# A fused hybrid block on one core: a bias added by VectorE, and sums of the expert units moved

## The chip, the core and the metric

The kernel runs on one core of a Trainium2 chip, as one program. The metric is the device time of one execution in microseconds; the kernel before takes 536.47 us, the median of 3 runs (535.53 to 536.54).

## The reference

One layer on 512 tokens of width 1024, all in float32:

```
mod = silu(c) @ w_ada + b_ada                  # 6 vectors of 1024: sh_a, sc_a, g_a, sh_f, sc_f, g_f
h   = rms_norm(x) * (1 + sc_a) + sh_a
proj = h @ w_in                                # -> conv value, conv gate, c_q, c_kv, k_rope
y_conv = silu(layer_norm(depthwise_conv31(val * sigmoid(gate))))
y_attn = attention(q, k, v from c_q, c_kv; 8 heads, chunk-causal)
x   = x + g_a * (concat(y_conv, y_attn) @ w_out)
h2  = rms_norm(x) * (1 + sc_f) + sh_f
y   = sum over the 2 chosen of 32 experts: gate_e * (silu(h2 @ Wg_e) * (h2 @ Wu_e)) @ Wd_e
out = x + g_f * y
```

`mod` is the conditioning; its last 4096 values (g_a, sh_f, sc_f, g_f) are what the first part of the change touches. The experts' weights are 3 MB each, 32 experts.

## The kernel before

Order. From the end of the first stage on, TensorE, VectorE, ScalarE and (until the experts) GpSimd run in the order in which the program text issues their instructions, and so does SyncE's queue of DMA triggers. A DMA that ScalarE triggers stands in ScalarE's order with its computations.

Stages. First the input projection of all tokens (`sweep1`). Then, while the convolution is prepared, the rest of the conditioning is computed in steps between other work: `ada_rest` (L569) makes two groups of 2048 values. A group is 8 products of the replicated silu(c) with a 128x2048 slice of `w_ada`, each as four products of 512 columns at four row positions of one PSUM bank (L574), then the bias as four more products of an identity column with the row tile `brow` (L581; a float32 product shows as two instructions, so 8 per group), then ScalarE copies the bank to a tile (L586). SyncE stores the four rows (L602) and reads them back in other shapes. `load_brow` (L565) is a DMA that ScalarE triggers; the first stands in the program after GpSimd's splittings of w_q_b and w_kv_b (L549, L552) and before the convolution's pairs, the second right after the first group's bias products. The `w_ada` slices come through a ring of 4 buffers.

The bank comes from the tag `f`, which has 2 buffers. Just before the first group, `conv_pair(1)` holds both: value and gate of a convolution tile. `conv_in` (L308) reads the gate with ScalarE's tanh (L312) and then the value with VectorE (L315). VectorE meanwhile works through the convolution's taps (L346).

`ada_rest`'s steps are called by `fill`: the first group's first step follows the first quarter of `conv_pair(2)`, its last step stands ahead of the last quarter's rest of `conv_pair(3)`; the second group runs between the q, k, v products and transpositions.

Then attention, the output projection with routing, and the experts. The experts' tokens are worked in 12 units of up to 128 rows (`Unit`, L1412), 2 or 4 experts each. A unit: transposition of the gathered rows (L1425), gate and up products (`gate_up`, L1451), silu and multiplication (L1454, L1456), transposition of the result (`turn`, L1463, copied by ScalarE at L1465), down products (`down`, L1477), scaling by gate and g_f with a split in a high part (ScalarE, L1481) and a low part (L1482), for two halves of 512 columns. `combine` (L1485) adds finished units to the residual: 8 steps, each a few products with a one-hot matrix into a bank (L1495) and a VectorE sum (L1498); with `store`, the result goes out by DMA (L1500), by SyncE and ScalarE in turn. From unit 5 on (`SOON`), four steps of the unit before stand in the middle of `gate_up`, four after `turn`. Before `turn` stands the next unit's transposition with its VectorE work (L1439, L1440). SyncE streams all weights (L1008) through 4 and 15 buffers and waits where a buffer is still read.

Of the kernel before, what the change touches and what calls it, by code (L numbers as in the profile page):

```python
# [12 lines left out]
F32 = mybir.dt.float32  # L13
# [4 lines left out]
OP = mybir.AluOpType  # L18
# [23 lines left out]
def hybrid_block(ctx: ExitStack, tc: tile.TileContext, A, out, dbg=None, stop=None):  # L42
    nc = tc.nc
    pe, act, dve, pool, sp = nc.tensor, nc.scalar, nc.vector, nc.gpsimd, nc.sync
# [42 lines left out]
    def nm(s):  # L87
        uid[0] += 1
        return f"{s}_{uid[0]}"
# [4 lines left out]
    def S(shape, dt=F32):  # L94
        return slots.tile(shape, dt, tag="s", name=nm("s"))

    def T(shape=(128, 512), dt=F32):
        return tmp.tile(list(shape), dt, tag="t", name=nm("t"))
# [4 lines left out]
    def acc(shape=(128, 512), dt=F32):  # L103
        return psum.tile(list(shape), dt, tag="acc", name=nm("acc"), bufs=4)

    def fb(shape=(128, 512), dt=F32):
        return psum.tile(list(shape), dt, tag="f", name=nm("f"), bufs=2)
# [4 lines left out]
    def C(shape, dt=F32, name=None, uname=None):  # L112
        return const.tile(list(shape), dt, tag=name, name=uname or name)
# [31 lines left out]
    def xrow(tt):  # L145
        return X[tt // 2][:, tt % 2, :]
# [23 lines left out]
    ident = C([128, 128], name="ident")  # L170
# [30 lines left out]
    def crep(j):  # L201
        return cs[:, j:j + 1].to_broadcast([128, 32])
# [62 lines left out]
    def sweep1(j):  # L265
        q, jj = j // 2, j % 2
        wh, wl = whl[q]
        hh, hl = hTh[j // 4][:, j % 4, :], hTl[j // 4][:, j % 4, :]
        for a in range(2):
            cc = slice(a * 128, (a + 1) * 128)  # L270
            mm3(pcv[a], wh[:, jj, cc], wl[:, jj, cc], hh, hl, j == 0, j == 7)
            yield
        for tt in range(4):
            cc = slice(tt * 128, (tt + 1) * 128)
            mm3(pcc[tt][:, :416], hh[:, cc], hl[:, cc], wh[:, jj, 256:], wl[:, jj, 256:], j == 0, j == 7)
            yield

    def run(g, n=100):
        for _ in range(n):
            if next(g, 0) == 0:  # L280
                break
# [5 lines left out]
    rp = S([128, 2048])  # L287
# [162 lines left out]
    for j in range(8):  # L450
        g = sweep1(j)
# [42 lines left out]
    def load_next():  # L494

        n = stream[0]
        stream[0] += 1
        if n < 16:
            t = ada_f[n // 8, n % 8] = W([128, 2048])
            sp.dma_start(t, w_ada[:, n % 8, 2048 + 2048 * (n // 8):4096 + 2048 * (n // 8)])  # L500
        elif n < 20:
            part, hf = (n - 15) % 2, (n - 16) // 2
            t = wout[part, hf] = W([128, 4, 512])
            sp.dma_start(t, wov[:, 4 * part:4 * part + 4, 512 * hf:512 * hf + 512])
# [11 lines left out]
    for tt in range(4):  # L516
        p = pcc[tt]
# [5 lines left out]
    for tt in range(4):  # L523
        p = pcc[tt]
# [34 lines left out]
    H2n = C([128, 8], name="H2n")  # L559
    rows = [dram.tile([4, 512], F32, tag=f"row{i}", name=f"row{i}") for i in range(2)]  # L560

    brow = rp[:4, 1536:2048]

    def load_brow(i):
        act.dma_start(brow, A["b_ada"][0, 2048 + 2048 * i:4096 + 2048 * i].rearrange("(a b) -> a b", b=512))  # L565

    load_brow(0)

    def ada_rest():  # L569
        for grp in range(2):  # L570
            p = fb()
            for j in range(8):
                for g in range(4):
                    pe.matmul(p[32 * g:32 * g + 32, :], crep(j), ada_f[grp, j][:, 512 * g:512 * g + 512],  # L574
                              start=(j == 0), stop=False, tile_position=(0, 32 * g), skip_group_check=True)
                if j < 7:
                    load_next()
                    store_rows(stream[0])
                    yield
            for g in range(4):  # L580
                pe.matmul(p[32 * g:32 * g + 32, :], ident[:4, g:g + 1].to_broadcast([4, 32]), brow,  # L581
                          start=False, stop=True, tile_position=(0, 32 * g), skip_group_check=True)
            if grp == 0:
                load_brow(1)
            s = T()
            act.copy(s, p)  # L586
            load_next()
            rows_due.append((stream[0] + RD[grp], grp, s))
            yield
        store_rows(100)  # L590
        yield
        store_rows(200)
# [27 lines left out]
    def conv_pair(t):  # L620
        wh, wl = pair_w[t]
        pv = [acc(), acc()] if t > 1 else [fb(), fb()]
        for a in range(2):
            for j in range(8):
                yield
                mm3(pv[a], wh[:, a, j, :], wl[:, a, j, :], hTh[j // 4][:, j % 4, :], hTl[j // 4][:, j % 4, :], j == 0, j == 7)
        conv_in(t, pv[0], pv[1])
# [12 lines left out]
    g = conv_pair(1)  # L640
# [4 lines left out]
    g = conv_pair(2)  # L645
# [9 lines left out]
    g = conv_pair(3)  # L655
# [80 lines left out]
    def qkv_fill():  # L736
        for i in range(24):
            fill(FQ[i % len(FQ)])
            yield
# [64 lines left out]
    g = qkv_fill()  # L804
# [186 lines left out]
    for kind in ORDER:  # L991
        n_ = sum(k[0] == kind for k in units)
# [41 lines left out]
    ga, gf = gw[:, 0], gw[:, 1]  # L1034
# [283 lines left out]
    for tt in range(4):  # L1318
        step = lambda k=1, tt=tt: run(rs_[tt], k)
        places = lambda tt=tt: (place(tt, 0, routed[tt][5]), tt < 3 and by_expert(tt, 0, routed[tt][5]))  # L1320
        n = 5 * tt + (5 if tt < 3 else 8)
        for d, f in ((0, lambda tt=tt: x2_part(tt, 0)), (D0, step), (D1, step)):
            at(n + d, f)
        if tt < 3:
            n = 31 + 8 * tt
# [86 lines left out]
    class Unit:  # L1412
# [53 lines left out]

        def down(self, eng=pool):

            n = self.n
            self.yhl = S([128, 2, 1024], F32R)  # L1470
            for hf in range(2):
                hs = slice(512 * hf, 512 * hf + 512)
                o = acc()
                for c in range(2):
                    for o_, w_, i in self.pieces:
                        w = self.weights(i, "d")
                        pe.matmul(o[o_:o_ + w_, :], self.aT[:, n * c + o_:n * c + o_ + w_], w.t[:, c, hs],  # L1477
                                  start=(c == 0), stop=(c == 1), tile_position=(0, o_), skip_group_check=True)
                yf = T()
                dve.scalar_tensor_tensor(yf[:n], o[:n], self.gate, gf[:n, hs], op0=OP.mult, op1=OP.mult)  # L1480
                act.copy(self.yhl[:n, 0, hs], yf[:n])  # L1481
                eng.tensor_tensor(self.yhl[:n, 1, hs], yf[:n], self.yhl[:n, 0, hs].bitcast(F32), op=OP.subtract)  # L1482
                yield

    def combine(us, banks=(fb,) * 4, store=False):  # L1485

        for u_ in us:
            if not u_.ot:
                u_.one_hot()
        for hf in range(2):  # L1490
            for tt in range(4):
                o = banks[tt]()
                for m, u_ in enumerate(us):
                    for k in range(2):
                        pe.matmul(o, u_.ot[:u_.n, tt * 128:(tt + 1) * 128], u_.yhl[:u_.n, k, 512 * hf:512 * hf + 512],  # L1495
                                  start=(m == 0 and k == 0), stop=(m == len(us) - 1 and k == 1))
                xr = xrow(tt)[:, 512 * hf:512 * hf + 512]
                dve.tensor_tensor(xr, xr, o, op=OP.add)  # L1498
                if store:
                    (act if tt % 2 else sp).dma_start(out[0, tt * 128:(tt + 1) * 128, 512 * hf:512 * hf + 512], xr)  # L1500
                yield
# [34 lines left out]
    cur = start(0)  # L1536
# [5 lines left out]
    SOON = 5  # L1542
    comb, done, side, prev = iter(()), [], over_table(), None
    for n_ in range(len(units)):
        last = n_ == len(units) - 1
        cur.gate_up(lambda: n_ >= SOON and run(comb, 4))
        if n_ == 1:
            run(gate)
        nxt_u = start(n_ + 1)
        if nxt_u:  # L1550
            nxt_u.complete()
        if prev:
            run(prev.down())
            done.append(prev)
        cur.turn()
        if n_ < SOON:
            if len(done) == 2:
                comb, done = combine(done), []
            run(comb, 4)
        else:  # L1560
            run(comb)
            if done:
                run(combine(done))
            if last:
                comb = combine([cur], (fb, fb, tr, tr), True)
                cur.one_hot()
                run(cur.down(dve))
                run(comb)
                break
            run(cur.down())  # L1570
            comb, done = combine([cur]), []
        if n_ > 1:
            run(side, 1)
        r_ = [Wt[e, part].room for part in (0, 1) for e in units[n_][2]]
        if n_ < 3:
            r_.remove("s")
        if prev:
            r_ += [Wt[e, "d"].room for e in units[n_ - 1][2]]
        if n_ >= SOON:
            r_ += [Wt[e, "d"].room for e in units[n_][2]]  # L1580
        room += r_
        loads_upto(len(keys))
        prev, cur = cur if n_ < SOON else None, nxt_u
# [124 lines left out]
```

## Time and profile before

| | |
|---|---|
| median of 3 runs | 536.47 us |
| the profiled execution's own time | 534.46 us |
| its span, first to last instruction | 532.9 us |
| TensorE busy | 486.2 us (91%) |
| VectorE, ScalarE, GpSimd busy | 289.0, 178.3, 124.4 us |
| granted TensorE clock, mean | 0.984 of full speed |
| moved by DMA | 154.42 MB, 290 GB/s |

The profile names PE (TensorE), PEld (its weight loads), DVE (VectorE), ACT (ScalarE), POOL (GpSimd) and SP (SyncE); a q behind the name is the engine's queue. "tile<-tiles" names what is written and read; `f`, `acc` and `tr` are PSUM banks. A bracket at the end of a timeline row is idle time of that engine before the row, and what ended it.

### The profile page before, as it was taken

The page shows a single profiled execution, that of the slowest core. Times are in us where ns is not written, and L with a number is a line of the kernel's source. Part 1 is how long each engine was busy: PE and PEld are TensorE (multiplying, and loading weights), DVE is VectorE, ACT ScalarE, POOL GpSimd, SP SyncE. Part 2 cuts the span into 40 slices and gives each one's busy share as a digit, 9 for nine tenths or more (in the row PEclk, how much of TensorE's full clock was granted, in tenths as well). Part 3 has the DMA queues.
Part 4 walks back from the last instruction along what each step waited for, and adds up shares of the span by engine and source line. Part 5 has one row for each costly group of instructions (what it writes and reads, how often), then busy time and mean ns, then how long its engine had stood idle before and what let it go on. Part 6 is the DMA issues. An engine that isn't in the chain of part 4 may idle for free.

```text
span 532.9 us, 8170 instructions
## 1 busy us (share of the span) xinstructions
PE 486.2 (91%) x2891; PEld 272.9 (51%) x2891; DVE 289.0 (54%) x655; ACT 178.3 (33%) x389; POOL 124.4 (23%) x118
## 2 busy tenths in 40 slices
PE   4899999999999898999998999999998999999982
PEld 4768975535644365788874343444433333223331
DVE  2447779957948675551556233436455454133544
ACT  4232744016575556821534422111201212021110
POOL 2311580007654543200000113012120212001100
PEclk9989999999999989999999999999999999999997
DMA  8999539985960262276968999999999999999934
GB/s 270 302 320 310 156 122 325 368 330 174 247 228 9 73 237 92 75 271 220 361 197 321 292 355 371 317 405 413 398 415 408 411 413 411 410 417 409 414 162 164
DMA packets 57859, 154.42 MB, mean 290 GB/s; under 512 B 7337, under 2 KB 26937, under 8 KB 51664
## 3 DMA queue, kind: packets, MB, share of 16 engines
q1 hardware_dynamic: 53232, 143.89, 75.6%
q10 hardware_dynamic: 2688, 5.92, 3.0%
q0 software_dynamic: 1888, 4.00, 2.3%
q8 instruction: 25, 0.41, 0.3%
q14 instruction: 26, 0.21, 0.1%
HBM read 150.97 MB, written 4.77 MB: 292 GB/s over the span
## 4 chain that ended last, share of the span: by engine, by line
PE 69%; DVE 13%; DMA 6%; ACT 4%; SPq 3%; issue 2%; POOL 1%; DVEq 0%; ACTq 0%; POOLq 0%
PE acc L1451 18%; PE acc L1477 9%; PE f L1495 8%; PE acc L116 5%; PE acc L118 4%; PE acc L117 4%; DVE s L1498 3%; DVE dw L346 2%; PE f L334 2%; DMA s<-in_w_ada_dram 2%; PE tr L1425 2%; DMA w<-in_w_ada_dram 2%; PE f L574 2%; PE acc L899 2%; DMA xg<-t 2%
## 5 line engine op out<-in xcount | busy, mean ns | idle before, releaser
L1451 PE MATMUL acc<-s,gw 128*32 128x512 f32 (+1 forms) x408 | 92.5, 597 | 0.0
L1498 DVE TENSOR_TENSOR s<-s,f 128x512 f32<-128x512 f32 x76 | 49.6, 685 | 35.9 <-PE f L1495 35.9
L116 PE MATMUL acc<-s,s 128*128 128x512 f32 (+3 forms) x160 | 63.2, 395 | 1.0 <-DVE s L774 1.0
L1495 PE MATMUL f<-s,t 128*128 128x512 f32 x184 | 54.4, 425 | 8.8 <-DVE s L1498 5.4
L118 PE MATMUL acc<-s,s 128*128 128x512 f32 (+3 forms) x160 | 58.8, 368 | 0.0
L117 PE MATMUL acc<-s,s 128*128 128x512 f32 (+3 forms) x160 | 58.8, 367 | 0.0
L346 DVE SCALAR_TENSOR_TENSOR dw<-s,cwh,dw 128x512 f32<-128x512 f32 x60 | 49.8, 844 | 1.2
L1451 PEld LDWEIGHTS acc<-s,gw 128*32 128x32 f32 (+1 forms) x408 | 24.6, 122 | 46.7 <-issue 44.8
L1451 PE MATMUL acc<-w,gw 128*32 128x512 f32 (+1 forms) x120 | 48.2, 622 | 0.0
L1482 POOL TENSOR_TENSOR s<-t,s 128x512 fp32r<-128x512 f32 x22 | 28.2, 1281 | 85.1 <-ACT s L1481 79.1
L1495 PEld LDWEIGHTS f<-s,t 128*128 128x128 f32 x184 | 30.0, 188 | 33.0 <-DVE s L1498 16.9
L1477 PE MATMUL acc<-s,t 128*64 128x512 f32 (+1 forms) x184 | 44.5, 598 | 0.0
L1454 ACT ACTIVATE t<-acc 128x256 f32<-128x256 f32 x12 | 4.6, 384 | 111.5 <-PE acc L1451 111.5
L116 PEld LDWEIGHTS acc<-s,s 128*128 128x128 f32 x160 | 30.2, 189 | 14.8 <-issue 7.9
L1456 DVE TENSOR_TENSOR t<-t,acc 128x256 f32<-128x256 f32 x12 | 5.1, 421 | 58.4 <-ACT t L1454 58.4
L1481 ACT CAST s<-t 128x512 fp32r<-128x512 f32 x24 | 14.8, 618 | 63.7 <-DVE t L1480 56.7
L1409 POOL DMA_INDIRECT s<-xg,sidx x11 | 11.7, 1060 | 98.1 <-PE tr L1425 61.7
L118 PEld LDWEIGHTS acc<-s,s 128*128 128x128 f32 x160 | 30.1, 188 | 4.1
L117 PEld LDWEIGHTS acc<-s,s 128*128 128x128 f32 x160 | 30.2, 189 | 3.3 <-issue 0.2
L1480 DVE SCALAR_TENSOR_TENSOR t<-acc,rt,gw 128x512 f32<-128x512 f32 x24 | 18.0, 750 | 25.0 <-PE acc L1477 25.0
L871 ACT ACTIVATE t<-acc,sm,qs 128x128 f32<-128x128 f32 (+3 forms) x32 | 19.7, 616 | 21.6 <-DVE sm L869 18.4
L868 DVE TENSOR_REDUCE sm<-acc 128x1 f32<-128x128 f32 (+3 forms) x32 | 15.5, 486 | 19.8 <-PE acc L867 19.7
(311 smaller groups left out, 817.1 us busy)
## 6 DMA issues: line engine op xcount, KB each, us to landing
s<-in_w_gate_e_dram SPq DMA_DIRECT2D x49, 512.0 KB
s<-in_w_up_e_dram SPq DMA_DIRECT2D x49, 512.0 KB, 10.9
s<-in_w_down_e_dram SPq DMA_DIRECT2D x22, 1024.0 KB, 12.5
w<-in_w_ada_dram SPq DMA_DIRECT2D x16, 1024.0 KB, 8.4
w<-in_w_down_e_dram SPq DMA_DIRECT2D x10, 1024.0 KB, 5.0
w<-in_w_gate_e_dram SPq DMA_DIRECT2D x15, 512.0 KB
w<-in_w_up_e_dram SPq DMA_DIRECT2D x15, 512.0 KB, 9.2
s<-in_w_ada_dram SPq DMA_DIRECT2D x6, 1024.0 KB, 11.2
```

Of the source, the lines that this page charges most:

```text
L116: pe.matmul(o, lh, rh, start=start, stop=False)
L117: pe.matmul(o, lh, rl, start=False, stop=False)
L118: pe.matmul(o, ll, rh, start=False, stop=stop)
L346: dve.scalar_tensor_tensor(dw[:, t, :], u[:, t // 2, k:k + 512], w, dw[:, t, :], op0=OP.mult, op1=OP.add)
L868: dve.tensor_reduce(H["mx"][:, qt:qt + 1], p[:, :n], axis=AX.X, op=OP.max)
L871: act.activation(e[:, :n], p[:, :n], AF.Exp, scale=qs[:, qt, h:h + 1], bias=H["nb"][:, qt:qt + 1], accum_out=H["rs"][:, qt:qt + 1])
L1451: pe.matmul(gu[sl, :], self.hg[:, j, sl], w.t[:, :, j % 4, :], start=(j == 0), stop=(j == 7), tile_position=(0, o_), skip_group_check=True)
L1477: pe.matmul(o[o_:o_ + w_, :], self.aT[:, n * c + o_:n * c + o_ + w_], w.t[:, c, hs], start=(c == 0), stop=(c == 1), tile_position=(0, o_), ...
L1480: dve.scalar_tensor_tensor(yf[:n], o[:n], self.gate, gf[:n, hs], op0=OP.mult, op1=OP.mult)
L1482: eng.tensor_tensor(self.yhl[:n, 1, hs], yf[:n], self.yhl[:n, 0, hs].bitcast(F32), op=OP.subtract)
L1495: pe.matmul(o, u_.ot[:u_.n, tt * 128:(tt + 1) * 128], u_.yhl[:u_.n, k, 512 * hf:512 * hf + 512], start=(m == 0 and k == 0), stop=(m == len ...
L1498: dve.tensor_tensor(xr, xr, o, op=OP.add)
```

## The change

Three edits. (1) The bias: `brow` becomes a tile of 128 partitions, set to zero by GpSimd; the four rows of the bias are loaded to partitions 0, 32, 64 and 96 of it; the four bias products of each group are gone; VectorE adds bank and `brow` into the tile that ScalarE's copy made. (2) From unit 5 on, two of the four steps of `combine` that stood after `turn` stand before it. (3) In the last unit, the second half's down products and scaling, then two steps of its own `combine`, stand ahead of the second half's low part; the second of its four banks comes from `acc` and not from `f`. `down` is cut into three functions for that.

```diff
-    brow = rp[:4, 1536:2048]
+    brow = rp[:, 1536:2048]
+    pool.memset(brow, 0.0)
 
     def load_brow(i):
-        act.dma_start(brow, A["b_ada"][0, 2048 + 2048 * i:4096 + 2048 * i].rearrange("(a b) -> a b", b=512))
+        act.dma_start(brow[0:128:32, :], A["b_ada"][0, 2048 + 2048 * i:4096 + 2048 * i].rearrange("(a b) -> a b", b=512))
 
     load_brow(0)
...
                     pe.matmul(p[32 * g:32 * g + 32, :], crep(j), ada_f[grp, j][:, 512 * g:512 * g + 512],
-                              start=(j == 0), stop=False, tile_position=(0, 32 * g), skip_group_check=True)
+                              start=(j == 0), stop=(j == 7), tile_position=(0, 32 * g), skip_group_check=True)
...
-            for g in range(4):
-                pe.matmul(p[32 * g:32 * g + 32, :], ident[:4, g:g + 1].to_broadcast([4, 32]), brow,
-                          start=False, stop=True, tile_position=(0, 32 * g), skip_group_check=True)
+            s = T()
+            dve.tensor_tensor(s, p, brow, op=OP.add)
             if grp == 0:
                 load_brow(1)
-            s = T()
-            act.copy(s, p)
             load_next()
...
         def down(self, eng=pool):
             self.yhl = S([128, 2, 1024], F32R)
             for hf in range(2):
+                self.products(hf)
+                self.scaled(hf)
+                self.low(hf, eng)
                 yield
...
+        if n_ >= SOON:
+            run(comb, 2)
         cur.turn()
...
             if last:
-                comb = combine([cur], (fb, fb, tr, tr), True)
+                comb = combine([cur], (fb, acc, tr, tr), True)
                 cur.one_hot()
-                run(cur.down(dve))
+                parts = cur.down(dve)
+                run(parts, 1)
+                cur.products(1)
+                cur.scaled(1)
+                run(comb, 2)
+                cur.low(1, dve)
                 run(comb)
                 break
```

`products` holds the down products of one half, `scaled` the VectorE scaling (L1480) and ScalarE's high part (L1481), `low` the subtraction (L1482).

## Rows read from the trace of the kernel before

**Rows 1.** Page, the chain that ended last: share of the span by engine.

```profile
PE 69%; DVE 13%; DMA 6%; ACT 4%; SPq 3%; issue 2%; POOL 1%; DVEq 0%; ACTq 0%; POOLq 0%
```

**Rows 2.** Timeline of PE, 76 to 109 us: start, length, engine, line, operation.

```profile
76.89 1.06 PE L574 MATMUL f<-w,cs 128*32 128x512 f32 x8
...
81.90 1.06 PE L574 MATMUL f<-w,cs 128*32 128x512 f32 x8 [0.60 <-DMA w<-in_w_ada_dram]
...
99.84 1.06 PE L574 MATMUL f<-w,cs 128*32 128x512 f32 x8 [1.33 <-DMA w<-in_w_ada_dram]
...
108.76 1.06 PE L581 MATMUL f<-s,ident 4*32 4x512 f32 x8
```

**Rows 3.** Timeline of ACT, 69 to 86 us.

```profile
69.94 0.52 ACTq L565 DMA_DIRECT2D s<-in_b_ada_dram  x1
...
75.02 0.60 ACT L312 ACTIVATE t<-f 128x512 f32<-128x512 f32 x1 [2.17 <-PE f L118]
83.15 0.36 ACTq L316 DMA_DIRECT2D ud<-t  x1
83.55 2.00 ACT L367 CAST s<-w 128x1024 fp32r<-128x1024 f32 x2 [7.94 <-DVE t L315]
```

**Rows 4.** Timeline of POOL, 76 to 80, 202 and 222 us.

```profile
76.78 2.83 POOL L552 TENSOR_TENSOR s<-w,s 128x1024 fp32r<-128x1024 f32 x1
...
202.12 0.36 POOL L1026 MEMSET rt<- 128x320 f32 x1 [2.22 <-ACT s L882]
...
222.30 1.81 POOL L1310 MEMSET s<- 128x2048 f32 x1 [7.69 <-PE acc L899]
```

**Rows 5.** Timeline of DVE, 82 to 151 us.

```profile
82.44 0.68 DVE L315 SCALAR_TENSOR_TENSOR t<-t,f 128x512 f32<-128x512 f32 x1
...
120.29 0.69 DVE L753 TENSOR_REDUCE sm<-t 128x8 f32<-128x512 f32 x1 [6.56 <-ACT t L750]
...
150.64 0.69 DVE L774 TENSOR_TENSOR s<-acc,ks 128x512 f32<-128x512 f32 x1 [3.07 <-POOL ks L193]
```

**Rows 6.** Windows: stretch, length, PE, PEld, DVE, ACT, POOL busy, PE clock, DMA, GB/s.

```profile
98.00:100.00 2.00, 0.67 (x7) 0.25 (x9) 2.00 (x4) 0.00 (x0) 0.00 (x0) 1.00 1.00 414
...
291.00:292.00 1.00, 1.00 (x5) 0.44 (x6) 0.85 (x2) 1.00 (x3) 0.03 (x1) 0.50 0.47 45
340.00:345.00 5.00, 5.00 (x28) 2.06 (x26) 1.80 (x3) 1.89 (x5) 1.02 (x1) 1.00 0.76 208
345.00:350.00 5.00, 5.00 (x24) 2.71 (x21) 2.88 (x4) 1.51 (x3) 2.56 (x2) 1.00 1.01 380
505.00:510.00 5.00, 4.81 (x36) 1.46 (x36) 1.75 (x3) 0.03 (x1) 0.00 (x0) 1.00 0.97 401
```

**Rows 7.** Timeline of PE, 289 to 300 us, the first unit.

```profile
289.13 0.24 PE L1196 MATMUL tr<-rt,ones 32*32 32x32 f32 x2 [1.50 <-DVE rt L1193]
...
291.01 5.16 PE L1451 MATMUL acc<-w,gw 128*64 128x512 f32 x16
295.97 3.63 PE L1451 MATMUL acc<-s,gw 128*64 128x512 f32 x16
```

**Rows 8.** Timeline of DVE and PE, 443 to 447 us, one later unit.

```profile
443.89 0.69 DVE L1440 TENSOR_TENSOR gw<-gw,H 128x512 f32<-128x512 f32 x1
...
446.84 0.62 PE L1477 MATMUL acc<-s,t 128*32 128x512 f32 x1
```

**Rows 9.** Timeline of DVE and PEld, 510 to 525 us, the last unit.

```profile
510.38 0.42 DVE L1456 TENSOR_TENSOR t<-t,acc 128x256 f32<-128x256 f32 x1 [3.40 <-ACT t L1454]
...
514.19 0.14 PEld L1477 LDWEIGHTS acc<-w,t 128*32 128x32 f32 x2 [0.23 <-DMA w<-in_w_down_e_dram]
...
518.18 0.74 DVE L1480 SCALAR_TENSOR_TENSOR t<-acc,rt,gw 128x512 f32<-128x512 f32 x1
519.61 0.69 DVE L1482 TENSOR_TENSOR s<-t,s 128x512 fp32r<-128x512 f32 x1 [0.69 <-ACT s L1481]
520.22 1.28 DVE L1498 TENSOR_TENSOR s<-s,f 128x512 f32<-128x512 f32 x2
```

More of the change, by code (lines that the diff above doesn't have):

```diff
@@ L1467, in down, with products, scaled, low @@
         def down(self, eng=pool):
-            n = self.n
             self.yhl = S([128, 2, 1024], F32R)
             for hf in range(2):
[L1472 to L1482, printed above, removed]
-                yield
+                self.products(hf)
+                self.scaled(hf)
+                self.low(hf, eng)
+                yield
+        def products(self, hf):
+            n = self.n
+            self.o = acc()
+            for c in range(2):
+                for o_, w_, i in self.pieces:
+                    w = self.weights(i, "d")
+                    pe.matmul(self.o[o_:o_ + w_, :], self.aT[:, n * c + o_:n * c + o_ + w_], w.t[:, c, 512 * hf:512 * hf + 512],
+                              start=(c == 0), stop=(c == 1), tile_position=(0, o_), skip_group_check=True)
+        def scaled(self, hf):
+            n = self.n
+            hs = slice(512 * hf, 512 * hf + 512)
+            self.yf = T()
+            dve.scalar_tensor_tensor(self.yf[:n], self.o[:n], self.gate, gf[:n, hs], op0=OP.mult, op1=OP.mult)
+            act.copy(self.yhl[:n, 0, hs], self.yf[:n])
+        def low(self, hf, eng):
+            n = self.n
+            hs = slice(512 * hf, 512 * hf + 512)
+            eng.tensor_tensor(self.yhl[:n, 1, hs], self.yf[:n], self.yhl[:n, 0, hs].bitcast(F32), op=OP.subtract)
     def combine(us, banks=(fb,) * 4, store=False):
```

## Prediction

> **What bounds the kernel now.** First the page's chain: TensorE holds 69% of it and VectorE 13% [rows 1]. So an edit counts by what it does to TensorE's row of work, and one on VectorE or ScalarE only where TensorE waits for it. Second the timeline of TensorE from 76 to 109 us, where the bias stands. It is without a gap but for two waits for a `w_ada` slice: 0.60 us before the second product of the first group, 1.33 us before the sixth [rows 2]. These are the only cushions after the first product: later than it by less than their sum costs nothing. Third the windows of the experts: the DMA engines' share is 0.76 at 340 to 345 us, 1.01 from 345 on and still 0.97 at 505 to 510, at 380 to 401 GB/s [rows 6]. Up to about 341 us buffers that TensorE frees pace the stream of weights; behind that the stream sets its own pace. Last the tail: the last unit's down product waits 0.23 us at 514.19 for its weights [rows 9]; behind it comes a chain of down products, scaling, splitting, sums and stores that nothing covers.
>
> So a delay of TensorE before 341 us moves everything after it one for one. A gain between 345 us and the last down product is worth nothing unless the stream ends earlier too. A gain in the tail counts in full.
>
> **Edit 1, the bias: what the new memset does to ScalarE's queue.** Before, the first `load_brow` waits for nothing: its trigger goes out at 69.94 us, ahead of the tanh L312 at 75.02 [rows 3]. After, it writes into a tile that GpSimd zeroes, and so waits for the memset. The memset stands in GpSimd's order behind L549 and L552, and L552 runs from 76.78 to 79.61 [rows 4]. For the length of a 128x512 memset I have 0.36 us for 128x320 and 1.81 for 128x2048 [rows 4]; between them by size 0.36 + 192/1728 x 1.45 = 0.52. It ends near 80.1. The trigger itself takes 0.52 at most [rows 3], so near 80.5 to 80.6 ScalarE's queue goes on.
>
> Behind the trigger stands L312, 0.60 us long. That a waiting trigger holds the computations behind it is shown by the next one: L316's trigger waits for VectorE's L315 (82.44 + 0.68), goes out at 83.15, and the cast behind it starts at 83.55 after 7.94 us idle [rows 3, 5]. So L312 moves from 75.02 to about 80.6 and ends at 81.2.
>
> Who waits for L312? The tag `f` has two banks, and `conv_pair(1)` holds both. The bank with the value is read by L315, only at 82.44 [rows 5]; the first conditioning product starts at 76.89 [rows 2], so it uses the bank that L312 reads. It can't start before 81.2: 81.2 - 76.89 = **+4.3 us** of idle TensorE, in order with all that follows. (Bounds of this term: 0, if the trigger doesn't hold L312; 5.0, if memset and trigger cost what their dearest rows say less what the queue overlaps.) L315 itself, at 82.44, keeps its place: L312's tile is there at 81.2. The margin is 1.2 us, so VectorE's taps don't move.
>
> The two slice waits take their part: the slices were on the way, so 0.60 + 1.33 = **-1.93** comes back at the second and sixth product [rows 2].
>
> TensorE's clock is the uncertain term. After 1.33 us of idle time in 98 to 100 us the granted clock was 1.00 (2.4 GHz) [rows 6]. After 1.50 us idle before 289.13, in a stretch of small waits, it was 0.50 (1.2 GHz), and 16 products took 5.16 us where the next 16 took 3.63 [rows 6, 7]: a loss of 1.53. An idle 4.3 us is longer than both. Bounds: 0, and 3.0 (twice the row's loss, if a low stretch lasts twice as long); I take the second row, **+1.5**. Of the two rows, the idle time of 4.3 us is nearer to 1.50 than to 1.33, and it is unbroken.
>
> The Trainium skill, in "TensorE: Matmul & The Clock Gate", section "What's actually happening", has it that the throttled state is the default and that activity is what releases it. The trace's 0.50 behind the waits at 289 us agrees; its 1.00 behind the wait at 98 shows that not every gap counts. By the rule the clock falls here; by the 98 us row alone it doesn't, and the sum below would be 1.5 less.
>
> **Edit 1: what is taken away.** Eight bias instructions per group of 128x512 (L581), 1.06 us in the row, of which the next instructions overlap a little, so 0.99 [rows 2]. Nothing releases them but the products before, so they are on TensorE's row. Two groups: **-0.99 -0.99 = -1.98**. For the second group I use the same price, since its instructions have the same form.
>
> **Edit 1: what is added.** VectorE's addition of a bank and a tile, 128x512, twice. The nearest rows are L774 and L1440, 0.69 us each [rows 5, 8]. The first falls behind 109.8 us (the products end there), ahead of 6.56 us of VectorE's idle time at 120.29; the second before the 3.07 idle us at 150.64 [rows 5]. What hides them are these gaps, so 0; without them it would be at most 2 x 0.69 = 1.4. Against that two ScalarE copies go. The first group's `load_brow(1)` now waits for the addition, as does SyncE's store of the rows (L602) instead of waiting for the copy; behind the store stand slices of the second group, read much later. I cost these waits at 0; bounds -0.2 and +0.7 (one addition late). The memset beside VectorE's work I cost at 0, bounds 0 and 0.5 (its own length).
>
> **Edit 2, two steps of `combine` before `turn`.** In five units (6 to 10) these steps filled the time after the transposition; now they fill TensorE's wait for VectorE's L1440 and the silu. In the unit at 444 us, L1440 ends at 444.58, two sums at a pitch of 0.6 follow, and the down products would start near 446.5 where they stand at 446.84 [rows 8]: 0.3 per unit, 1.65 for five. The last unit waits 3.40 us for the silu at 510.38 [rows 9], and two steps ahead (two products of some 0.5) bring its first down product 1.06 us forward. Together 2.7 us. But the last weights land near 514.2 and TensorE waits for them already [rows 9]; the stream runs at 0.97 to 1.01 [rows 6]. So it counts **0**, and TensorE stands idle 2.4 us longer before the last down products. Bounds -2.7 (the stream ends earlier too) and 0.
>
> That new idle time is where the clock could fall a second time, with 4 us of down products and sums behind it. Bounds 0 and 1.5 (by the 289 us row); I take **+1.0**.
>
> **Edit 3, the last unit's halves.** Before: L1480 of the second half ends at 518.92, its low part L1482 waits 0.69 us for ScalarE's cast, and four pairs of sums of 1.28 us follow at a pitch of 1.2, the last ending at 520.22 + 3 x 1.2 + 1.28 = 525.1, with the first pair's product held until both halves are done [rows 9]. After, the first half's sums stand in the wait for the cast: the first sum can start at 518.97 in place of 520.2, the low part comes behind two of them, and the six others follow at 0.6 to 0.7 us or TensorE's pace. The last one ends near 524.5: **-0.55**. Bounds -1.3 (all of the sums' lead) and +0.7 (the low part, one VectorE instruction later, sets the second half's products). Stores and what ends the program come behind the last sum as before: 532.9 - 525.1 = 7.8 us.
>
> **Sum.** +4.3 - 1.93 + 1.5 - 1.98 + 0 + 1.0 - 0.55 = **+2.3 us**. The trace's span is 532.9, its own time 534.46, and the median of the runs 536.47, 2.01 above it. The forecast is 536.8 by the profiled execution's measure, 538.8 by the median's.
>
> **Rivals.** R1, the stall comes and TensorE's clock holds through both idle stretches: without 1.5 and 1.0 the sum is -0.2, 536.3. For it: clock 1.00 after 1.33 us idle [rows 6]. Against it: 0.50 after 1.50 [rows 6, 7], and three times that length here.
>
> R2, the other side, clearly faster: the trigger doesn't hold L312. One mechanism: the trigger has left, or is passed, before L312's bank is needed. It decides at about 76.3 us, when memset and trigger would have to be done for L312 to end by 76.89. Then 4.3, 1.93 and the first 1.5 fall away: -1.98 - 0.55 + (0 to 1.5) = -2.5 to -1.0, so 534.0 to 535.5, middle 534.9. For it: nothing but that the trace holds no trigger of ScalarE waiting for GpSimd. Against it: L316 and the cast behind it [rows 3].
>
> R3, the gain in the experts counts: the stream ends earlier because two steps ahead free buffers, and so no second fall of the clock: 4.3 - 1.93 + 1.5 - 1.98 - 0.55 - 2.7 = -1.4, 535.1. For it: 0.97 is not 1.0 [rows 6]. Against it: 1.01 from 345 us on.
>
> **How the numbers follow.** Forecast 0.60 (537.4 to 540.5 as its own range: clock 0 to +3 at the stall, the tail's bounds), R1 0.17, R2 0.13, R3 0.10. About 0.2%, 1.07 us, is what a measurement of this kernel can tell from no change: faster is below 535.40, slower above 537.54. R1 is mostly within (0.15 of 0.17), R2 all but faster (0.12), R3 splits (0.05, 0.05); of the forecast 0.58 lie above. That is faster 0.19, same 0.21, slower 0.60, rounded. The range reaches from 535.2, which cuts R2's better half and some of R3, to 541.0, the forecast's upper bounds.
>
> **What would show it.** In the trace after: GpSimd's memset right behind L552, ScalarE's L565 trigger at about 80.2, L312 at 80.6, and the first L574 at 81.2 with some 4 us idle, released by ScalarE (R2 if it stays near 77). No wait for a slice at the second and sixth product, or a shorter one. A granted clock of 0.5 for some microseconds behind 81 us (R1 if it stays 1.00). No L581. The last unit's down product waits 2 to 3 us for `w_down_e` (R3 if it doesn't and starts before 514), and then a clock below 1. The last L1498 ends about 7.8 us before the end. I am wrong in the main thing if TensorE has no new idle time at 77 us.

## The result and the profile after

The changed kernel takes 538.82 us (median of 17 runs, 534.84 to 542.15), the kernel before 535.62 in the same comparison: ratio 1.0059, 95% interval 1.0038 to 1.008. Beside later experiments it was 538.52 against 536.63, ratio 1.0016 (0.9986 to 1.0046). So it is slower, as forecast, by 3.2 us in the first comparison, clear of noise, and by 1 (ratio) to 2 us (medians) in the second, whose interval includes no change. The profiled execution has a span of 535.6 us and a time of its own of 537.18, 2.7 us over that of before.

The place the forecast hung on is the queue of ScalarE. GpSimd, ScalarE and TensorE of the changed kernel, one fence each (L563 is the zeroing, L566 the trigger of the bias's rows, L575 the conditioning's product); they answer to [rows 2 to 4]:

```profile
77.25 2.79 POOL L552 TENSOR_TENSOR s<-w,s 128x1024 fp32r<-128x1024 f32 x1
79.98 0.52 POOL L563 MEMSET s<- 128x512 f32 x1
```

```profile
72.26 1.06 ACT L551 CAST s<-w 128x1024 fp32r<-128x1024 f32 x1
80.53 1.10 ACTq L566 DMA_DIRECT2D s<-in_b_ada_dram  x1
81.74 0.60 ACT L312 ACTIVATE t<-f 128x512 f32<-128x512 f32 x1 [8.42 <-issue]
83.57 0.34 ACTq L316 DMA_DIRECT2D ud<-t  x1
```

```profile
82.39 1.82 PE L575 MATMUL f<-w,cs 128*32 128x512 f32 x8 [4.96 <-ACT t L312]
84.13 1.12 PE L630 MATMUL tr<-ident,t 128*128 128x128 f32 x4
...
88.32 1.06 PE L575 MATMUL f<-w,cs 128*32 128x512 f32 x8
...
104.90 1.06 PE L575 MATMUL f<-w,cs 128*32 128x512 f32 x8
...
112.78 1.92 PE L575 MATMUL f<-w,cs 128*32 128x512 f32 x16
```

The reader sees the chain in four steps. The zeroing waits for its turn behind L552. The trigger goes out when the zeroing is done. The tanh, which had its data at 75 us in the kernel before, starts when the trigger has been issued; the bracket says "issue", since nothing that the profile shows holds ScalarE itself. TensorE stands idle for 4.96 us, released by the tanh. The waits for slices are gone at the second and sixth product (88.32 and 104.90 have no bracket), and the last row of 16 instructions is two products in a row with no bias between them.

The clock behind the stall, by windows of the changed kernel (stretch, length, PE, PEld, DVE, ACT, POOL busy, granted clock, DMA share, GB/s):

```profile
82.00:84.00 2.00, 1.61 (x8) 0.16 (x8) 1.97 (x4) 0.38 (x2) 0.00 (x0) 0.64 0.95 397
84.00:86.00 2.00, 2.00 (x11) 1.68 (x8) 1.92 (x3) 2.00 (x3) 0.00 (x0) 0.51 0.85 238
188.00:192.00 4.00, 2.45 (x16) 1.68 (x15) 3.93 (x9) 1.88 (x5) 2.96 (x3) 1.00 0.60 180
290.00:294.00 4.00, 2.41 (x21) 1.75 (x19) 2.69 (x15) 1.06 (x4) 0.35 (x1) 1.00 0.38 154
508.00:510.00 2.00, 2.00 (x24) 0.73 (x17) 0.00 (x0) 0.00 (x0) 0.00 (x0) 1.00 0.99 410
510.00:512.00 2.00, 2.00 (x11) 0.78 (x5) 0.24 (x1) 0.39 (x1) 0.00 (x0) 1.00 0.79 324
512.00:514.00 2.00, 1.84 (x8) 0.80 (x6) 1.77 (x4) 0.37 (x1) 0.00 (x0) 1.00 0.36 147
514.00:516.00 2.00, 2.00 (x7) 0.28 (x6) 1.29 (x3) 0.00 (x0) 0.00 (x0) 1.00 0.11 45
516.00:518.00 2.00, 0.56 (x9) 0.19 (x12) 0.00 (x0) 0.00 (x0) 0.00 (x0) 1.00 0.03 12
```

After 5 us without a product the clock is at its lower level, 1.2 GHz, until about 86 us: the first eight instructions take 1.82 us where they took 1.06 [rows 2]. The same windows of the kernel before show what the sum did not have:

```profile
188.00:192.00 4.00, 3.81 (x28) 3.04 (x28) 3.44 (x8) 2.27 (x7) 2.81 (x3) 0.57 0.52 182
290.00:294.00 4.00, 4.00 (x16) 1.99 (x17) 1.98 (x11) 3.47 (x10) 1.72 (x2) 0.58 0.60 169
508.00:510.00 2.00, 1.81 (x20) 0.30 (x12) 0.00 (x0) 0.03 (x1) 0.00 (x0) 1.00 0.90 373
510.00:512.00 2.00, 1.14 (x6) 0.84 (x6) 0.62 (x2) 0.72 (x2) 0.00 (x0) 1.00 0.58 238
512.00:514.00 2.00, 1.69 (x8) 0.74 (x10) 1.77 (x4) 0.00 (x0) 0.00 (x0) 1.00 0.20 82
514.00:516.00 2.00, 2.00 (x23) 0.75 (x21) 1.00 (x3) 0.00 (x0) 0.00 (x0) 1.00 0.03 8
```

Two low stretches, near 190 and 291 us, are in the profiled execution of before and not in that of after. And the stream of weights, which has one pace in both (about 410 GB/s), does not end at once: its share falls from 0.9 to nothing over some 5 us in the kernel before and 8 in the changed one, so ever less of the 16 DMA engines' time is in use (which engines, the windows don't show). A share of 0.03 in the last window is half of one engine's time, of 16.

The last unit of the changed kernel, TensorE and VectorE (L1480 the down products, L1487 the scaling, L1493 the low part, L1508 the sums); they answer to [rows 9]:

```profile
512.83 1.33 PE L1505 MATMUL f<-s,t 128*128 128x512 f32 x4 [0.16 <-DVE s L1508]
514.10 1.98 PE L1480 MATMUL acc<-s,t 128*32 128x512 f32 x6
517.51 0.62 PE L1480 MATMUL acc<-w,t 128*32 128x512 f32 x1 [1.44 <-DMA w<-in_w_down_e_dram]
```

```profile
520.89 0.69 DVE L1493 TENSOR_TENSOR s<-t,s 128x512 fp32r<-128x512 f32 x1 [0.69 <-ACT s L1488]
521.50 0.74 DVE L1487 SCALAR_TENSOR_TENSOR t<-acc,rt,gw 128x512 f32<-128x512 f32 x1
522.17 0.69 DVE L1508 TENSOR_TENSOR s<-s,f 128x512 f32<-128x512 f32 x1
522.78 0.68 DVE L1508 TENSOR_TENSOR s<-s,acc 128x512 f32<-128x512 f32 x1
523.38 0.68 DVE L1493 TENSOR_TENSOR s<-t,s 128x512 fp32r<-128x512 f32 x1
...
526.37 1.28 DVE L1508 TENSOR_TENSOR s<-s,tr 128x512 f32<-128x512 f32 x2
```

The product that needs the last weights waits 1.44 us (its weight load 2.35) and starts at 517.51 in place of 514.2. From there to the last sum's end it is 10.14 us (517.51 to 527.65), before 10.9 (514.2 to 525.1): two sums stand where VectorE waited for ScalarE's second cast.

### The profile page after: what moved, and what is told of

Read it like the earlier page. It is cut to its first block, busy times and chain, and to the rows that moved or that the text cites. A ratio compares the mean times of both kernels' runs of the same rounds, so it can differ in the third digit from the quotient of the medians.

```text
span 535.6 us, 8141 instructions
## 1 busy us (share of the span) xinstructions
PE 484.7 (91%) x2875; PEld 272.7 (51%) x2875; DVE 289.9 (54%) x657; ACT 177.7 (33%) x387; POOL 124.3 (23%) x119
## 4 chain that ended last, share of the span: by engine, by line
PE 69%; DVE 11%; DMA 7%; ACT 4%; SPq 3%; POOL 2%; issue 2%; ACTq 0%; DVEq 0%; POOLq 0%
PE acc L1449 17%; PE acc L1480 9%; PE f L1505 7%; PE acc L116 6%; PE acc L117 5%; PE acc L118 5%; DMA w<-in_w_down_e_dram 3%; PE f L575 3%; DVE s L1508 2%; PE f L334 2%; DMA s<-in_w_ada_dram 2%; PE tr L1423 2%; SPq L167 2%; DMA xg<-t 2%; PE acc L865 2%
## 5 line engine op out<-in xcount | busy, mean ns | idle before, releaser
L1508 DVE TENSOR_TENSOR s<-s,f 128x512 f32<-128x512 f32 x74 | 48.4, 685 | 33.5 <-PE f L1505 33.5
L1493 POOL TENSOR_TENSOR s<-t,s 128x512 fp32r<-128x512 f32 x22 | 28.2, 1282 | 83.2 <-ACT s L1488 77.6
L1449 PE MATMUL acc<-w,gw 128*32 128x512 f32 (+1 forms) x120 | 47.0, 595 | 0.1
L1480 PE MATMUL acc<-s,t 128*64 128x512 f32 (+1 forms) x184 | 45.6, 599 | 0.0
L116 PEld LDWEIGHTS acc<-s,s 128*128 128x128 f32 x160 | 30.3, 189 | 14.9 <-issue 7.9
L1488 ACT CAST s<-t 128x512 fp32r<-128x512 f32 x24 | 14.9, 620 | 63.8 <-DVE t L1487 63.8
L1487 DVE SCALAR_TENSOR_TENSOR t<-acc,rt,gw 128x512 f32<-128x512 f32 x24 | 18.0, 750 | 28.1 <-PE acc L1480 28.1
L1480 PE MATMUL acc<-w,t 128*32 128x512 f32 (+1 forms) x80 | 26.0, 597 | 1.4 <-DMA w<-in_w_down_e_dram 1.4
```

Source lines behind the costliest of these rows:

```text
L116: pe.matmul(o, lh, rh, start=start, stop=False)
L1449: pe.matmul(gu[sl, :], self.hg[:, j, sl], w.t[:, :, j % 4, :], start=(j == 0), stop=(j == 7), tile_position=(0, o_), skip_group_check=True)
L1480: pe.matmul(self.o[o_:o_ + w_, :], self.aT[:, n * c + o_:n * c + o_ + w_], w.t[:, c, 512 * hf:512 * hf + 512], start=(c == 0), stop=(c == ...
L1487: dve.scalar_tensor_tensor(self.yf[:n], self.o[:n], self.gate, gf[:n, hs], op0=OP.mult, op1=OP.mult)
L1493: eng.tensor_tensor(self.yhl[:n, 1, hs], self.yf[:n], self.yhl[:n, 0, hs].bitcast(F32), op=OP.subtract)
```

## The experiments

Theory A is the forecast's: the trigger that waits in ScalarE's queue is what costs, and the rest of the change gives back some 2.5 us. The rival B: the delay at 77 us is given back, and the loss arises at the end of the stream. Eight kernels were made, three of them ran twice, and the changed kernel ran once more: twelve experiments of 6 to 12 runs each, in three groups on three chips, each group beside its own runs of the kernel before (535.83, 536.91 and 536.63 us). A ratio goes with the runs on its own chip; medians of different groups come from different chips, and which chip the first comparison ran on is not known.

| kernel | median, us | ratio to before (95%) |
|---|---|---|
| early zeroing, all three edits | 534.54 | 0.9979 (0.9953 to 1.0005) |
| early zeroing, edits 1 and 3 | 534.52 | 0.9969 (0.9947 to 0.9992) |
| early zeroing, edit 1 | 534.96 | 0.9976 (0.9951 to 1.0001) |
| trigger later, all three edits | 535.38 | 0.998 (0.9949 to 1.001) |
| changed kernel without edit 2 | 538.97 | 1.0053 (1.0027 to 1.0079) |
| changed kernel without edit 3 | 541.61; 539.98 | 1.0091 (1.0063 to 1.0118); 1.0056 (1.0025 to 1.0087) |
| edit 1 alone | 541.21; 540.92 | 1.0116 (1.0075 to 1.0156); 1.0074 (1.0041 to 1.0106) |
| before with the wait alone | 540.9; 540.98 | 1.0091 (1.0062 to 1.0121); 1.0082 (1.0056 to 1.0109) |

The first four have no stall, the last four have it.

**Zeroing early.**

```diff
         pool.memset(zz, 0.0)
+        pool.memset(rp[:, 1536:2048], 0.0)
...
-    pool.memset(brow, 0.0)
```

> The changed kernel with GpSimd's zeroing moved to the convolution's set-up, tens of microseconds before the trigger needs it. Theory A (the wait of ScalarE's trigger is what costs): TensorE has no idle time ahead of the first conditioning product and no low clock behind it; the two slice waits of 0.60 and 1.33 us return. 4.96 + 1.5 - 1.93 = 4.5 us less, about 534.3. Theory B (the delay at 77 us is given back later, and the longer time arises at the end of the stream of expert weights): the last w_down lands within 1 us of where it does in the changed kernel, and the time is 538 or more.

534.54 us, 4.3 below the changed kernel's 538.82 (and 0.8% by the ratios). Theory A gave 534.3. ScalarE's and TensorE's rows in this kernel (L313 is the tanh):

```profile
70.24 1.10 ACTq L566 DMA_DIRECT2D s<-in_b_ada_dram  x1
...
75.28 0.60 ACT L313 ACTIVATE t<-f 128x512 f32<-128x512 f32 x1 [2.15 <-PE f L118]
```

```profile
77.16 1.06 PE L575 MATMUL f<-w,cs 128*32 128x512 f32 x8
...
82.25 1.06 PE L575 MATMUL f<-w,cs 128*32 128x512 f32 x8 [0.69 <-DMA w<-in_w_ada_dram]
```

The trigger leaves before the tanh, the product starts without idle time, and the wait for a slice is back. The product that needs the last weights starts at 512.36 us, 5.2 us earlier than in the changed kernel's profile (517.51). Theory B falls by this and by its 538.

**The wait alone.**

```diff
     brow = rp[:4, 1536:2048]
+    pool.memset(rp[:, 1536:2048], 0.0)
```

> The kernel before with only the wait: GpSimd zeroes the columns of the bias's tile ahead of the first trigger, the four rows of the bias then land on it as before, and the 16 products stay. Theory A: 5 us of idle time at 77 us, a clock of 0.5 behind it, 1.93 us taken back at the slice waits: 535.6 + 4.5 = 540.1. Theory B: the delay is given back before the end; 535.6 to 536.6.

> The wait alone once more, on one chip with the three that follow. All theories: 4 to 5 us over the kernel before.

540.9 and 540.98, that is 5.1 and 4.4 over before on their chips; theory A had 4.5. Its rows show the chain without the rest of the change:

```profile
80.60 0.52 ACTq L566 DMA_DIRECT2D s<-in_b_ada_dram  x1
81.23 0.60 ACT L312 ACTIVATE t<-f 128x512 f32<-128x512 f32 x1 [7.84 <-POOL s L563]
```

Here the four rows go to partitions 0 to 3 and the trigger takes 0.52 us; with rows 32 partitions apart it takes 1.10.

**The trigger later.** The zeroing stays where the change put it; only the trigger's place in ScalarE's order differs.

```diff
-    load_brow(0)
...
+                if grp == 0 and j == 0:
+                    load_brow(0)
                 if j < 7:
```

> The changed kernel with GpSimd's zeroing where it is, and the first trigger of the bias issued after the first conditioning step, so that in ScalarE's order it stands behind the tanh L312. Theory A (the trigger's place ahead of L312 is the cause): no idle time at 77 us, the same time as the early zeroing, 534.5 within 0.8. Rival E (the zeroing beside VectorE's work, or its transfer, delays by itself): the first conditioning product stays late and the time is 538 or more.

535.38 us, 0.9 above 534.5 where theory A allowed 0.8; but the kernel before is 1.1 us slower in this group, and the ratio of 0.998 is the early zeroing's 0.9979. The zeroing runs at the same time as in the changed kernel, the tanh at 75, the trigger at 83.93 behind L316:

```profile
79.90 0.53 POOL L563 MEMSET s<- 128x512 f32 x1
```

```profile
75.34 0.60 ACT L312 ACTIVATE t<-f 128x512 f32<-128x512 f32 x1 [2.15 <-PE f L118]
83.49 0.35 ACTq L316 DMA_DIRECT2D ud<-t  x1
...
83.93 1.10 ACTq L566 DMA_DIRECT2D s<-in_b_ada_dram  x1
```

So it is the place of a waiting trigger in ScalarE's order, and neither the zeroing nor the transfer.

**Edit 2 undone, with the stall and without it.**

```diff
-        if n_ >= SOON:
-            run(comb, 2)
         cur.turn()
```

> The changed kernel with edit 2 undone: from unit 5 on all four steps stand behind the transposition again. Theory A: TensorE reaches the last down products about 1.8 us later and waits that much less for the last weights; the time is the same, 538.8 within 0.7. Theory B (edit 2 itself delays the last weights): the last w_down lands 2 us earlier and the time falls to about 536.5.

> Early zeroing with edit 2 undone (edits 1 and 3 remain). Theory A: the stream of weights sets the end, edit 2 is worth nothing: within 0.7 of the early zeroing with edit 2, 534.5. Rival D (two steps ahead of the transposition count on TensorE's row): 1.65 more, about 536.2.

538.97 beside the changed kernel's 538.82, and 534.52 beside 534.54, both across groups: edit 2 is worth nothing that these runs can tell, as forecast, and rival D's 1.65 us is not there. With edit 2 the last unit waits longer for its weights: 1.44 us in the early zeroing, 0.80 without edit 2:

```profile
512.36 0.62 PE L1480 MATMUL acc<-w,t 128*32 128x512 f32 x1 [1.44 <-DMA w<-in_w_down_e_dram]
```

```profile
515.41 0.62 PE L1480 MATMUL acc<-w,t 128*32 128x512 f32 x1 [0.80 <-DMA w<-in_w_down_e_dram]
```

**The bias alone, with the stall and without it** (edits 2 and 3 undone; in the second also the early zeroing).

> The changed kernel with edits 2 and 3 undone, so the bias's edit alone with its wait. Theory A: the wait alone cost 5.1 us by the runs' medians and 4.75 by the traces; less 1.98 for the 16 products that is +2.8 to +3.1 against before, about 538.8. Rival C (the products' removal is given back, as the slices of w_ada set the pace there): 540.5 or more.

> The bias's edit alone with its wait, once more. Theory A (its 16 products leave TensorE's row whether or not the wait is there): 1.98 us below the wait alone on this chip. Rival F (with the wait, TensorE's idle time at the end or another clock fall eats their removal): equal to the wait alone within 0.7.

> Early zeroing, edit 1 alone. Theory A: the 16 products' removal counts in full, 535.8 - 2.0 = 533.8, and against the early zeroing with all edits +0.8 for the old tail (534.5 + 0.8 = 535.3); so 533.8 to 535.3. Rival C: 535.8, no gain against before.

Without the stall 534.96 against 536.91, inside theory A's 533.8 to 535.3: 2.0 us less by the medians, 1.3 by the ratio 0.9976, whose interval ends just above 1; rival C had no gain. With the stall 541.21 (six runs, 536.33 to 544.54) and 540.92, beside 540.9 and 540.98 for the wait alone: no gain at all in the medians, where 1.98 was expected. It was a miss of theory A: 541.21 is what rival C gave, 540.92 what rival F gave. By the intervals, 0.3 to 0.4% on either side, 1.98 us (0.37%) is not excluded in the pair on one chip (540.92 and 540.98); in the other, across chips, it is, narrowly.

The traces settle where the gain is not lost. The wait alone and the bias alone with its wait, one fence each, from TensorE's stall to the first product behind the second group:

```profile
81.96 1.74 PE L575 MATMUL f<-w,cs 128*32 128x512 f32 x8 [4.42 <-ACT t L312]
...
147.51 0.50 PE L116 MATMUL acc<-s,s 128*128 128x512 f32 x1
```

```profile
82.01 1.93 PE L575 MATMUL f<-w,cs 128*32 128x512 f32 x8 [4.95 <-ACT t L312]
...
145.17 0.50 PE L116 MATMUL acc<-s,s 128*128 128x512 f32 x1
```

From the start of the idle time (77.54 and 77.06) that is 69.97 us with the products and 68.11 without them; in the other pair of traces it is 70.45 and 68.44. Without the stall the same stretch takes 63.9 to 64.1 us in all four kernels, and 65.98 in the kernel before. So the 16 products leave TensorE's row in full by 150 us, with the stall and without it, and rival C's reason, that the slices of `w_ada` give them back there, falls. What the medians lack is lost later, or is noise.

**The old tail.**

```diff
-                comb = combine([cur], (fb, acc, tr, tr), True)
+                comb = combine([cur], (fb, fb, tr, tr), True)
...
+                run(cur.down(dve))
+                run(comb)
```

> The changed kernel with edit 3 undone. Theory A: the stretch from the first product that waits for the last weights to the end of the last sum goes from 10.1 back to 10.9 us, and the time from 538.8 to 539.5. Rival: the tail's new order hides nothing, both stretches are equal and the time is 538.8.

> The changed kernel with the old tail once more. Theory A: 0.76 over the changed kernel on this chip, equal to the bias alone within 0.7. Rival G: 2.3 or more over the changed kernel.

> The changed kernel once more. Theory A: below the bias alone by the tail's 0.76, edit 2 being worth nothing. Rival G (edit 3 is worth more than its stretch shows): 2.3 or more below.

The stretch from the product that waits for the last weights to the last sum's end is 10.90 us in the first profile of this kernel (518.28 to 529.18) and 10.13 in the changed kernel's second profile (514.73 to 524.86): 0.77 apart, as in the first pair. In the runs the old tail is 2.8 (across groups) and 1.5 us slower by the medians, 1.7 and 2.1 by the ratios, with intervals of about 0.3% on each ratio. Two other pairs on one chip bear on it. The changed kernel is 2.4 us below the bias alone (538.52 and 540.92), which is rival G's figure and not theory A's 0.76; 0.9 of that lies between the bias alone and the old tail, which theory A had equal within 0.7. Without the stall, edits 1 and 3 are 0.4 us below edit 1 alone (534.52 and 534.96). The sign is the same each time, no pair of ratios is clear of noise by itself, and the size is not settled between 0.4 and rival G's 2.3. The other profile of the changed kernel is of use beside it:

```profile
82.43 1.59 PE L575 MATMUL f<-w,cs 128*32 128x512 f32 x8 [4.95 <-ACT t L312]
```

```profile
514.73 0.62 PE L1480 MATMUL acc<-w,t 128*32 128x512 f32 x1 [1.44 <-DMA w<-in_w_down_e_dram]
```

The stall is the same to 0.01 us, and the last weights are there 2.8 us earlier than in the first profile of the same kernel. The span of this second profile is 532.9 us, that of the kernel before, with the stall in it: one profile alone would not have shown the loss.

## Why the prediction was right, and where only its sum was

To set the terms against the trace, I take the distance of the two kernels at like places of their chains of waits, less the 0.47 us by which the changed kernel's profile was late already when the input projection ended (77.43 against 76.96):

| place | changed minus before, us | step |
|---|---|---|
| first conditioning product | +5.03 | the stall; forecast +4.3 |
| second product | +5.95 | clock +1.52 (forecast +1.5), slice wait -0.60 |
| sixth product | +4.59 | slice wait -1.36 (forecast -1.33) |
| behind the first group | +3.42 | bias and neighbours -1.17 (forecast -0.99) |
| behind the second group | +2.47 | bias -0.95 (forecast -0.99) |
| end of attention, 270 us | +1.42 | low clock near 190 us absent, -1.05; not forecast |
| behind the first unit's first products | +0.53 | a transfer 0.55 longer, low clock near 291 us absent; not forecast |
| unit before last, 499 us | -1.27 | edit 2's steps -1.8 (forecast -1.65, to be lost again) |
| first product with the last weights | +2.84 | the last weights' trigger +3.05; not forecast |
| last sum's end | +2.09 | tail -0.75 (forecast -0.55) |
| end of the program | +2.2 | |

The mechanism was right at each of its steps up to 150 us; the conditioning's products started late for the reason given, and the slices and the clock took the parts given. Of the stall's 0.7 us too little, 0.58 is the trigger: I gave it the 0.52 us of the row of before, and to partitions 32 apart it takes 1.10. The kernel with the wait alone, whose trigger takes 0.52, has a stall of 4.37.

The step that failed is the last +1.0, a second fall of the clock in the new idle time before the last down products: the granted clock was 1.00 there in both profiles of the changed kernel, though TensorE had work for only 0.56 of 2.00 us in 516 to 518. The wait itself came, 1.44 us on TensorE's row and 2.35 on its weight loads where 2 to 3 were forecast. Edit 2 was costed at nothing for the right reason, the stream sets the end.

That the trace's sum, +2.2, meets the forecast's +2.3 is partly luck. The absent low stretches took about 2.5 us off, and the stream of weights put 2.3 back, at the same pace of bytes. SyncE's triggers show where; the last four of the stream, before and after:

```profile
495.20 2.88 SPq L1008 DMA_DIRECT2D s<-in_w_down_e_dram  x3
499.03 0.33 SPq L1008 DMA_DIRECT2D w<-in_w_down_e_dram  x1
```

```profile
497.22 4.38 SPq L1006 DMA_DIRECT2D s<-in_w_down_e_dram  x3
502.55 0.33 SPq L1006 DMA_DIRECT2D w<-in_w_down_e_dram  x1
```

Less the 0.47, the triggers stood 0.51 us apart at 372 us, 1.55 at the first of these and 3.05 at the last. The last transfer was no slower: from its trigger to the product that needs it took 15.0 us, before 15.2. The last 1.5 us arose within these four, where SyncE stood 2.2 us, by the profile's waits, for an earlier slice of gate weights to land (before 0.7); why that one came late stays open. In the second profile of the changed kernel the last trigger goes out at 499.62, so this delay does not repeat; the absence of the low stretches does.

The median's hit, 538.82 where 538.8 was forecast, is luck too: the forecast started from 536.47, and beside the 17 runs the kernel before takes 535.62, so that the difference is +3.2 and not +2.3.

What repeats is the difference between kernels with the stall and without it in the medians: 538.82 against 534.54 and 538.97 against 534.52 (across groups; 0.80% and 0.84% by the ratios), 540.9 and 540.98 against 535.83 and 536.63 on their own chips, which is 4.3 to 5.1 us. The bias alone, with its wait and without it on one chip, is 6.3 apart (541.21 and 534.96), with the spread of the first as said. The forecast's own terms for the wait, 4.3 - 1.93 + 1.5, made 3.9.

Of the rivals, R1 (the clock holds) falls by the 0.64 and 0.51 behind the stall; in the second idle time the clock did hold, as R1 had it. R2 (no stall) falls by the first fence. R3's gain in the experts falls by the two pairs with and without edit 2. R2's time is what the kernel takes once the wait is gone, as far as the medians go: -2.5 to -1.0 was its range, and the four kernels without the stall lie 1.3 to 2.4 us below before, though the interval of only one of them ends below 1. Two slips of the working changed nothing: by its bounds R2's middle is 534.7 and not 534.9, and the shares listed add up to 0.58 slower and 0.23 same, where 0.60 and 0.21 stand.

What stays open: where behind 150 us the gain of the 16 products goes beside the stall, if it is not noise; whether edit 3 gives 0.4 or 2 us; and what makes the last triggers late in one execution and not in another. Runs of one kernel spread by 4 to 10 us here, more than any of these. The lowest ratio of the study is that of the early zeroing with edits 1 and 3, 0.9969 (0.9947 to 0.9992); edit 2 can be left out.

## What to carry to other kernels

A DMA trigger is an instruction in its engine's order. Before it is made to wait for anything, read what stands behind it in that engine's queue and who waits for that; issuing it a few instructions later, or making its condition true early, can cost nothing where the wait costs 4 us. Work saved while a saturated stream sets the end is only waiting time moved, and a sum of terms should be tested term by term, since a single profile of such a kernel carries chance of 2 to 3 us: the two of the changed kernel have spans of 535.6 and 532.9.

## What the runs showed of the hardware

A first trigger of four rows took 0.52 us to adjacent partitions (three profiles) and 1.10 us to partitions 32 apart (eleven profiles), the second of the same form 0.28 and 0.52 to 0.53: twice as long for the spread rows.

The clock's low stretches come and go between executions of one kernel: near 190 and 291 us the profile of before has both (clock 0.57 and 0.58), both profiles of the changed kernel have neither, and that of the bias alone in the third group has both (mean clock 0.73 in 188 to 194, 0.72 in 292 to 298). Of the fourteen profiles eleven have both; the three with neither are those two and the bias alone's other one (1.00 in both windows). All three have the stall, as have six of the eleven, so it is not shown whether the stall has a part in their absence. Over the changed kernel's 17 runs the mean granted clock goes with the time (correlation -0.72). The Trainium skill, "TensorE: Matmul & The Clock Gate", section "What's actually happening", has it that what the clock follows runs free and does not restart with the kernel, so that the same kernel changes clock at different points. The traces agree in that one stage runs at either level in different executions; what the clock follows they do not show.

The stream of weights does not end at once. From a full share to the last weights' landing 5 to 8 us pass in the two profiles shown, and the changed kernel's last weights come at 517.5 after 3.5 us at a share of 0.11 and then 0.03, worth less than two of the sixteen engines. When they come goes with their trigger: in all fourteen profiles the last unit's weight load waits for them and starts 14.9 to 15.8 us after SyncE's last trigger, which itself goes out anywhere from 497.4 to 507.4 us.
